# GpSimd arithmetic moved to VectorE, unsplit side tasks, and scores of two heads as 64-row products

## The chip, the core and the metric

One NeuronCore of a Trainium2 chip runs the whole program as one launch. The metric is the device time of that launch in microseconds (us). Engines are named as in the profile: PE is TensorE (PEld its weight loads), DVE is VectorE, ACT is ScalarE, POOL is GpSimd, SP is SyncE, which issues DMAs. "L292" is line 292 of the kernel before.

## The reference, cut

Two blocks over 256 tokens of width 1024, in float32. The first has two layers (a mixer of three kinds of attention, then an MLP of width 4096). The second has a Hyena layer and an attention layer, each followed by 16 experts. What the change touches is in the second block and in what is computed ahead for it:

```python
def hyena_filters(L, w1, b1, w2, b2, w3, freq):        # 64 hidden units
    ...
    h = (h @ w3).reshape(L, HY_ORDER, 2, D_MAIN)       # 2 orders, 2 directions, 768 channels
    h = h * jnp.exp(-t * jnp.abs(deltas))
    h = h / (jnp.sum(jnp.abs(h), axis=(0, 2), keepdims=True) + 1e-6)
    ...                                                # then an FFT of the taps
def memory_cross_attn(cq, mem_n, w_kv):                # 4 heads of 64, 256 memory rows
    mk, mv = jnp.split(mem_n @ w_kv, 2, axis=-1)
    s = jnp.einsum('bqhd,bmhd->bhqm', q, mk) * (HEAD_DIM ** -0.5)
    return jnp.einsum('bhqm,bmhd->bqhd', jax.nn.softmax(s, axis=-1), mv)
def blocked_gqa(q, k, v):                              # 12 query heads of 64 on 4 key heads
    s = jnp.einsum('bqhgd,bkhd->bhgqk', qblk, k) * scale
    return jnp.einsum('bhgqk,bkhd->bqhgd', jax.nn.softmax(s, axis=-1), v)
```

The Hyena layer (`long_conv`) multiplies spectra of 256 tokens with spectra of these filters; both second-block layers add a cross attention over the normalized memory.

## The kernel before, in words

**Stages.** By time in the trace: first mixer to 232 us, its MLP (MLP 0) to 508, second mixer to 752, MLP 1 to 936, Hyena layer to 1086, first experts to 1399, attention layer to 1526, second experts to the end at 1870.8.

**Split products.** Most matrix products run as three passes on a fast number format, fp32r (`mm3`, L304 to L306): each f32 operand is split into hi (rounded, by ACT, L291) and lo (the rest, a subtraction, L292). L292 takes its engine from a cycle: `LO0` in MLP 0 and MLP 1, `LO1` in the Hyena layer, `LO2` in the attention layer's projections, `LO3` in its output projection; all of them alternate between POOL (`G`) and DVE (`V`). The first block's mixers use DVE alone. A few products run in plain f32: the scores and the probabilities of the second block's attention. The trace shows each as two PE instructions.

**Order.** `Pipe.feed` (L112) prepares a unit of weights (load, split) two units ahead of its products; each time a unit has run, `Pipe.tick` (L101) steps every spawned task once. While MLP 0 runs, such a side task computes the filters (`filters_task`, L1063) and then the memory's keys and values (`memory_task`, L1161), and writes them to DRAM (`kd`, `kvd`). A scheduler then reorders instructions on each engine, and every engine works through its own queue in order.

**Filters.** For four parts (order by half of the channels) and two token tiles, two directions each take one product of 128 rows with the weights' hi part and one of 64 rows with the lo part (L1122, L1123) into one PSUM tile `psf`; DVE multiplies by the decay (L1124), POOL adds absolute values into `sab` (L1130), DVE forms sum and difference (L1135), ACT and POOL split them into `hs` (L1136, L1137). PE adds the absolute values up (`psn`, L1142), and three-pass products with the split constant `fFh`, `fFl` give the spectra.

**Memory.** `Norm` (L344 to L373) transposes a tile (`pst`), splits it into `xh` (ACT) and `xl` (DVE, L348), and makes the row of reciprocal norms from `ms`, `nr` and `nrb` (DVE, L360 to L366), which PE spreads over partitions (`psr`, L371). The keys (`psT`) and values (`psM`) are three-pass products fed by the generator `stream`.

**Hyena layer.** Projections as three-pass products, short convolutions on DVE (`ux`, `uv`), then forward transform (`psz`), a complex product with `kd` split into `yh` (ACT) and `yl` (DVE or POOL), inverse transform (`psy`), the gate, and the split output `ah`, `al`; L1372 to L1375, L1380 and L1401 may run on POOL.

**Attention layer.** `main` and `cross_task` run `attend` (L1192) for pairs of heads, in rounds staggered against one another, while PE also does the projections. The keys of a pair stand block-diagonally in `akb` (or `mkb`), 128 rows by two heads of 256 keys, with zeros elsewhere, so that one product of 128 rows by 512 columns gives the scores of both heads for 128 queries (`psl`, L1197). A softmax (`softmax_pair`, L769 to L790) follows, four transposes per key half (`pst`, L1207), and the product with the values (`psv`, L1215). Score, transpose and value tiles share one PSUM pool `B` of four buffers. Rotary turns are on POOL and DVE. The projections run in the order key and last query columns (512 to 1023), cross query, first query columns (0 to 511), values.

## Time and profile before

| | |
|---|---|
| median of 3 runs | 1873.15 us (1870.21 to 1873.5) |
| the profiled execution's own time | 1872.64 us |
| its span in the trace | 1870.8 us |
| mean granted PE clock | 0.959 |
| PE busy | 1628.8 us (87%), 11139 instructions |
| DVE busy | 985.2 us (53%), 1740 |
| ACT busy | 676.6 us (36%), 1118 |
| POOL busy | 315.1 us (17%), 216 |
| DMA in the chain that ended last | 30%, all of it expert weights |

Busy shares are means over stages with different limits: the two expert stages wait for weights, and the mixers and MLPs keep PE busy nearly all the time. So each stage has to be read by itself. The time of an execution is some 2 us more than its span.

### The profile page before, as it was taken

How to read it: one execution, taken by the hardware profiler on the slowest of the kernel's cores; microseconds unless marked ns; L12 is line 12 of the kernel's file. 1: busy time of each engine (PE TensorE's matmuls, PEld its weight loads, DVE VectorE, ACT ScalarE, POOL GpSimd, SP SyncE). 2: the span in 40 equal slices, each digit the busy share in tenths (PEclk: the TensorE clock that was granted, in tenths of full speed). 3: DMA queues.
4: the chain of work that ended last, by engine and by line, in shares of the span. 5: the costliest groups of instructions: out<-in, count | busy, mean ns of one | idle time of the engine just before them, and what ended most of it. 6: DMA issues, size and time to landing. Idle time of an engine off the chain costs nothing. (4 is left out here: it accounts for less than half of the span.)

```text
span 1870.8 us, 27208 instructions
## 1 busy us (share of the span) xinstructions
PE 1628.8 (87%) x11139; PEld 1195.2 (64%) x11139; DVE 985.2 (53%) x1740; ACT 676.6 (36%) x1118; POOL 315.1 (17%) x216
## 2 busy tenths in 40 slices
PE   8999999998999999999989988666667989776765
PEld 7998977788999989999878844212224655221221
DVE  6998686775579977645578752000006862110102
ACT  6446454554454555544445331000003652000001
POOL 1000026654300000444333300000002210000001
PEclk9999999999999999999999988898989999899888
DMA  7543564454644436755244689999998759999997
GB/s 257 160 137 125 172 201 160 164 203 161 209 142 147 130 124 203 278 185 196 99 153 157 254 353 425 425 426 424 426 405 315 272 203 401 425 425 425 425 421 274
DMA packets 136516, 490.41 MB, mean 262 GB/s; under 512 B 11153, under 2 KB 32068, under 8 KB 115912
## 3 DMA queue, kind: packets, MB, share of 16 engines
q1 hardware_dynamic: 135919, 488.11, 69.2%
q8 instruction: 87, 1.43, 0.3%
q10 hardware_dynamic: 472, 0.57, 0.1%
q14 instruction: 38, 0.30, 0.0%
HBM read 483.41 MB, written 5.24 MB: 261 GB/s over the span
## 5 line engine op out<-in xcount | busy, mean ns | idle before, releaser
L291 ACT ACTIVATE hi<-w 128x1024 fp32r<-128x1024 f32 (+3 forms) x330 | 328.0, 997 | 323.7 <-PE psT L306 162.3
L304 PE MATMUL psT<-xh,hi 128*128 128x256 f32 x1328 | 386.8, 291 | 0.9 <-ACT hi L291 0.9
L305 PE MATMUL psT<-xh,lo 128*128 128x256 f32 x1328 | 378.6, 285 | 4.6 <-POOL lo L292 2.7
L306 PE MATMUL psT<-xl,hi 128*128 128x256 f32 x1328 | 378.7, 285 | 0.0
L292 DVE TENSOR_TENSOR lo<-w,hi 128x1024 fp32r<-128x1024 f32 (+3 forms) x245 | 285.3, 1165 | 141.5 <-ACT hi L291 140.6
L292 POOL TENSOR_TENSOR lo<-w,hi 128x1024 fp32r<-128x1024 f32 (+1 forms) x85 | 205.0, 2413 | 590.2 <-ACT hi L291 584.6
L305 PEld LDWEIGHTS psT<-xh,lo 128*128 128x128 f32 x1328 | 256.4, 193 | 9.5 <-POOL lo L292 3.3
L304 PEld LDWEIGHTS psT<-xh,hi 128*128 128x128 f32 x1328 | 256.5, 193 | 9.2 <-issue 6.4
L306 PEld LDWEIGHTS psT<-xl,hi 128*128 128x128 f32 x1328 | 256.1, 193 | 1.4 <-issue 1.1
L1741 PE MATMUL psx<-w,late 128*32 128x256 f32 (+1 forms) x1024 | 154.4, 549 | 75.8 <-DMA w<-in_exp_w_gate 39.5
L1741 PEld LDWEIGHTS psx<-w,late 128*32 128x32 f32 x1024 | 47.1, 116 | 180.5 <-issue 74.9
L1741 PE MATMUL psx<-w,xg 128*32 128x256 f32 (+1 forms) x1024 | 124.3, 547 | 35.2 <-DMA w<-in_exp_w_up 19.7
L1793 PE MATMUL psy<-w,late 128*32 128x512 f32 x576 | 98.8, 601 | 33.7 <-DMA w<-in_exp_w_down 29.8
L1777 ACT ACTIVATE yy<-psy,rslot 128x512 fp32r<-128x512 f32 (+1 forms) x17 | 11.3, 662 | 320.6 <-PE psy L1793 253.7
L1741 PEld LDWEIGHTS psx<-w,xg 128*32 128x32 f32 x1024 | 40.5, 117 | 115.7 <-issue 60.6
L306 PE MATMUL acc<-lo,hh 128*128 128x512 f32 x256 | 100.8, 394 | 3.0 <-POOL lo L292 3.0
L305 PE MATMUL acc<-hi,hlo 128*128 128x512 f32 x256 | 100.8, 394 | 0.0
L304 PE MATMUL acc<-hi,hh 128*128 128x512 f32 x256 | 100.5, 392 | 0.0
L1778 DVE SCALAR_TENSOR_TENSOR yy<-psy,rslot,yy 128x512 fp32r<-128x512 f32 (+1 forms) x17 | 12.2, 720 | 162.0 <-ACT yy L1777 161.5
L1757 DVE TENSOR_TENSOR late<-late,psx 128x512 f32<-128x512 f32 (+1 forms) x16 | 8.1, 550 | 166.3 <-PE psx L1741 166.3
L1793 PEld LDWEIGHTS psy<-w,late 128*32 128x32 f32 x576 | 27.1, 110 | 101.1 <-DMA w<-in_exp_w_down 49.8
L1756 DVE SCALAR_TENSOR_TENSOR late<-psx,rslot,late 128x512 f32<-128x512 f32 (+1 forms) x16 | 9.1, 613 | 152.3 <-ACT late L1755 152.3
(495 smaller groups left out, 2850.1 us busy)
## 6 DMA issues: line engine op xcount, KB each, us to landing
w<-in_exp_w_gate SPq DMA_DIRECT2D x64, 1536.0 KB, 27.6
w<-in_exp_w_up SPq DMA_DIRECT2D x64, 1536.0 KB, 29.5
w<-in_exp_w_down SPq DMA_DIRECT2D x48, 1536.0 KB, 26.9
w<-in_w_in SPq DMA_DIRECT2D x39, 1024.0 KB, 5.2
w<-in_w_up SPq DMA_DIRECT2D x32, 1024.0 KB, 5.6
w<-in_w_down SPq DMA_DIRECT2D x32, 1024.0 KB, 7.1
w<-in_exp_w_down SPq DMA_DIRECT2D x18, 1024.0 KB, 14.2
w<-in_w_out SPq DMA_DIRECT2D x10, 1024.0 KB, 5.6
```

The costliest lines, as they stand in the source:

```text
L291: S.activation(hi, src, AF.Copy)
L292: next(lo_engines[0]).tensor_tensor(lo, src, hi.bitcast(F32), op=ALU.subtract)
L304: PE.matmul(ps, lh, rh, start=start, stop=False)
L305: PE.matmul(ps, ll, rh, start=False, stop=False)
L306: PE.matmul(ps, lh, rl, start=False, stop=stop)
L1741: mm = PE.matmul(pg[nm][n][32 * e:32 * e + 32, :c1 - c0], xg[gr // 2][:, k, 128 * (gr % 2) + 32 * e:128 * (gr % 2) + 32 * e + 32], wt[e][: ...
L1756: V.scalar_tensor_tensor(sg[:, :n], pg["gate"][i][:, :n], r2, sg[:, :n], op0=ALU.mult, op1=ALU.mult)
L1757: V.tensor_tensor(hid[:, c], sg[:, :n], pg["up"][i][:, :n], op=ALU.mult)
L1777: S.activation(yh, py, AF.Copy, scale=rs[:, 2, gr:gr + 1])
L1778: V.scalar_tensor_tensor(yl, py, rs[:, 2, gr:gr + 1], yh.bitcast(F32), op0=ALU.mult, op1=ALU.subtract)
L1793: PE.matmul(py[n][32 * e:32 * e + 32], hT[:, k, 32 * e:32 * e + 32], wt[e][:, k - k0, 512 * n:512 * n + 512], start=k == 0, stop=k == 5, t ...
```

## The change

All `LO` cycles become DVE alone, and so do the Hyena layer's and the attention layer's remaining POOL operations; POOL keeps the routing of the experts and the last output. The side tasks keep their operands in f32: the filter taps become 64-row products, one direction in rows 0 to 63 of the array and one in rows 64 to 127 (`tile_position`), each into its own PSUM tile; the spectra and the memory's keys and values become plain f32 products, and the memory norm makes one f32 tile instead of `xh` and `xl`. In `attend`, one head's keys stand in rows 0 to 63 and the other's in 64 to 127; four products of 64 rows by 256 columns replace two of 128 by 512, and each head gets its own `psl` tile, so the softmax runs per head over both token tiles. The attention layer's first query projection comes before the load of the cross query's and values' weights.

The diff, cut ("LO" lines, `Norm`, `softmax_pair`, filters, memory, `attend`, Hyena layer, attention layer):

```diff
     lo_engines = [cycle((V,))]
-    LO0 = (G, V)
-    LO1 = (G, V)
-    LO2 = (V, G, V)
-    LO3 = (G, V)
+    LO0 = (V,)
...
+            if split is None:
+                self.x = pool.tile([128, 8, T], F32, name="xT")
+            elif split:
                 self.xh = (pool or xtp).tile([128, 8, T], F32R, tag="xh", name="xh")
                 self.xl = (pool or xtp).tile([128, 8, T], F32R, tag="xl", name="xl")
...
+                        S.activation(self.x[:, k], ps[:, j], AF.Copy, scale=self.g[:, k:k + 1])
+                        continue
                     S.activation(self.xh[:, k], ps[:, j], AF.Copy, scale=self.g[:, k:k + 1])
                     V.scalar_tensor_tensor(self.xl[:, k], ps[:, j], self.g[:, k:k + 1], self.xh[:, k].bitcast(F32),
...
-                V.tensor_scalar(nm[:, q:q + 1], nm[:, q:q + 1], scale[q], -1.0, op0=ALU.mult, op1=ALU.mult)
+            V.scalar_tensor_tensor(nm, nm, -1.0, scale, op0=ALU.mult, op1=ALU.mult)
+            scale = [scale[:, q:q + 1] for q in range(2)]
         for q in range(2):
             S.activation(p[:, q], ps[:, q], AF.Exp, bias=nm[:, q:q + 1], scale=scale[q], accum_out=sm[:, q:q + 1])
...
-            Fh = fp.tile([128, 2, 2, 128], F32R, name="fFh")
-            Fl = fp.tile([128, 2, 2, 128], F32R, name="fFl")
-            S.activation(Fh, raw, AF.Copy)
-            V.tensor_tensor(Fl, raw, Fh.bitcast(F32), op=ALU.subtract)
+            F = fp.tile([128, 2, 2, 128], F32, name="fF")
+            nc.sync.dma_start(F, C["fwd"].rearrange("p t (s f) -> p t s f", s=2)[:, :, :, :128])
             yield
...
-            S.activation(hst, h2, AF.Copy)
-            V.tensor_tensor(hst[64:], h2[64:], hst[64:].bitcast(F32), op=ALU.subtract)
...
-                        nc.sync.dma_start(w3[64 * d:64 * d + 64], I["hy_filt_w3_2"][0].rearrange("k (o d c) -> k o d c", o=2, d=2)[:, o, :, c])
...
-                    G.tensor_tensor(w3l, w3[:64], w3h[:64].bitcast(F32), op=ALU.subtract)
-                    hs = {op: [fp.tile([128, 2, 384], F32R, tag=f"h{op}{i}", name="hs") for i in range(2)] for op in (ALU.add, ALU.subtract)}
+                        nc.sync.dma_start(w3[64 * d:64 * d + 64], I["hy_filt_w3_2"][0].rearrange("k (o d c) -> k o d c", o=2, d=2)[:, o, d, c])
+                    hs = {op: fp.tile([128, 2, 384], F32, tag=f"h{op}", name="hs") for op in (ALU.add, ALU.subtract)}
                     sab = fp.tile([128, 384], F32, tag="sab", name="sab")
                     yield
                     for t in range(2):
                         hd = []
+                        sl = slice(t * 128, (t + 1) * 128)
+                        pd = [A("psf", [128, 384]) for _ in range(2)]
+                        for d in range(2):
+                            r = slice(64 * d, 64 * d + 64)
+                            PE.matmul(pd[d], h2[r, sl], w3[r], start=True, stop=True, tile_position=(64 * d, 0))
                         for d in range(2):
                             h = fp.tile([128, 384], F32, tag=f"hd{d}", name="hd")
-                            ps = A("psf", [128, 384])
-                            sl = slice(t * 128, (t + 1) * 128)
-                            PE.matmul(ps, hst[:, sl], w3h[:, d], start=True, stop=False)
-                            PE.matmul(ps, hst[:64, sl], w3l[:, d], start=False, stop=True)
-                            V.tensor_tensor(h, ps, dec[:, t, c], op=ALU.mult)
+                            V.tensor_tensor(h, pd[d], dec[:, t, c], op=ALU.mult)
                             if t == 0 and d == 0:
                                 S.activation(sab, h, AF.Abs)
...
-                                G.tensor_tensor(sab, sab, ab, op=ALU.add)
+                                V.tensor_tensor(sab, sab, ab, op=ALU.add)
                             hd.append(h)
                         yield
                         for op, dst in hs.items():
-                            x = fp.tile([128, 384], F32, tag="hx", name="hx")
-                            V.tensor_tensor(x, hd[0], hd[1], op=op)
-                            S.activation(dst[0][:, t], x, AF.Copy)
-                            G.tensor_tensor(dst[1][:, t], x, dst[0][:, t].bitcast(F32), op=ALU.subtract)
+                            V.tensor_tensor(dst[:, t], hd[0], hd[1], op=op)
...
-                            mm3(pp[t], Fh[:, t, part], Fl[:, t, part], hs[op][0][:, t], hs[op][1][:, t], True, True)
+                            PE.matmul(pp[t], F[:, t, part], hs[op][:, t], start=True, stop=True)
...
             kv = mp.tile([128, 2, 2, T], F32, name="kv")
             w = load(ring, rows_of(I["w_mem_kv_2"][l]))
             yield
-            def put_k(j, ps):
-                V.tensor_tensor(kv[:, 0], ps, nm.R[:, None, :].to_broadcast([128, 2, T]), op=ALU.mult)
-            def put_v(ps):
+            yield
+            ps = A("psT", [128, 2, T])
+            for i in range(2):
+                for q in range(2):
+                    for k in range(4):
+                        PE.matmul(ps[:, q], w[i][:, k, 128 * q:128 * q + 128], nm.x[:, 4 * i + k],
+                                  start=i == 0 and q == 0 and k == 0, stop=i == 1 and q == 1 and k == 3)
+                yield
+            V.tensor_tensor(kv[:, 0], ps, nm.R[:, None, :].to_broadcast([128, 2, T]), op=ALU.mult)
+            ps = [A("psM") for _ in range(2)]
+            for k0 in range(0, 8, 2):
                 for t in range(2):
...
-            yield from stream(dense_M(ring, None, nm.xh, nm.xl, put_v, tiles=[x[:, :, 256:] for x in w]), sp)
+                    for k in (k0, k0 + 1):
+                        PE.matmul(ps[t][:, :256], nm.x[:, k, t * 128:(t + 1) * 128], w[k // 4][:, k % 4, 256:],
+                                  start=k == 0, stop=k == 7)
+                yield
+            for t in range(2):
...
-        kb = pool.tile([128, 2, 2, T], F32, name="mkb")
+        kb = pool.tile([128, 2, 2, T], F32, name="mkb")[:, 0]
         vv = pool.tile([128, 2, 256], F32, name="mvv")
-        G.memset(kb, 0.0)
-        for q in range(2):
-            r = slice(64 * q, 64 * q + 64)
-            nc.sync.dma_start(kb[r, :, q], kvd[r, 0])
+        nc.sync.dma_start(kb, kvd[:, 0])
...
+        ps = [B("psl") for _ in range(2)]
+        for t in range(2):
+            for q in range(2):
+                r = slice(64 * q, 64 * q + 64)
+                PE.matmul(ps[q][:, t], qT[r, t * 128:(t + 1) * 128], kb[r], start=True, stop=True, tile_position=(64 * q, 0))
         p = []
-        for t in range(2):
-            ps = B("psl")
-            PE.matmul(ps, qT[:, t * 128:(t + 1) * 128], kb, start=True, stop=True)
-            pt = pool.tile([128, 2, T], F32, tag="p", name="p")
-            softmax_pair(ps, pt, scale(t), eng)
-            p.append(pt)
+        for q in range(2):
+            p.append(pool.tile([128, 2, T], F32, tag="p", name="p"))
+            softmax_pair(ps[q], p[q], scale(q), eng)
...
-                    PE.transpose(ps[:, q, t * 128:(t + 1) * 128], p[t][:, q, st * 128:(st + 1) * 128], ident)
+                    PE.transpose(ps[:, q, t * 128:(t + 1) * 128], p[q][:, t, st * 128:(st + 1) * 128], ident)
...
-            return attend(cqT[:, j], kv[0][:, j], lambda t: 0.125,
+            return attend(cqT[:, j], kv[0][:, j], lambda q: 0.125,
...
-                G.tensor_tensor(a[0], a[0], a[1], op=ALU.subtract)
+                V.tensor_tensor(a[0], a[0], a[1], op=ALU.subtract)
                 V.tensor_tensor(a[2], a[2], a[3], op=ALU.add)
...
-                    (G if part and not o else V).tensor_tensor(yl[:, b], a[2 * part], yh[:, b].bitcast(F32), op=ALU.subtract)
+                    V.tensor_tensor(yl[:, b], a[2 * part], yh[:, b].bitcast(F32), op=ALU.subtract)
...
-                    (V if n else G).tensor_tensor(al[:, b], sz, ah[:, b].bitcast(F32), op=ALU.subtract)
+                    V.tensor_tensor(al[:, b], sz, ah[:, b].bitcast(F32), op=ALU.subtract)
...
-        G.memset(kb, 0.0)
+        kb = late.tile([128, 2, T], F32, name="akb")
...
-                        G.tensor_tensor(hx(rot[:, t, a:a + 64 * nh])[:, :, :, g], hx(qk[:, t, a:a + 64 * nh])[:, :, :, 1 - g],
+                        V.tensor_tensor(hx(rot[:, t, a:a + 64 * nh])[:, :, :, g], hx(qk[:, t, a:a + 64 * nh])[:, :, :, 1 - g],
...
-                for c in range(2):
-                    V.tensor_copy(kb[0:64, c, 0], ps[0:64, c])
-                    S.activation(kb[64:128, c, 1], ps[64:128, c], AF.Copy)
+                V.tensor_copy(kb, ps)
...
         pipe.feed(dense_M(ring, w_in[:, :, 512:1024], nm.xh, nm.xl, lambda ps: qk_done(1, ps), need=need_r, tiles=wqk or None))
+        pipe.feed(dense_M(ring, w_in[:, :, 0:512], nm.xh, nm.xl, lambda ps: qk_done(0, ps)))
         w = load(ring, w_in[:, :, 1024:1536])
         kv = memory_load(pool, kvd)
...
         def cq_done(j, ps):
-            while nm.R is None:
-                pipe.tick()
...
         ct = pipe.spawn(cross_task(kv, cqT, late, lambda: "cq" in done, lambda: box.get("a"), E2))
         pipe.feed(dense_T(ring, None, nm.xh, nm.xl, cq_done, tiles=[x[:, :, 256:] for x in w]))
-        pipe.feed(dense_M(ring, w_in[:, :, 0:512], nm.xh, nm.xl, lambda ps: qk_done(0, ps)))
         pipe.spawn(main())
         pipe.feed(dense_M(ring, None, nm.xh, nm.xl, v_done, tiles=[x[:, :, :256] for x in w]))
```

**PE in MLP 0, a filter group between the products of the MLP** (`psT` is the MLP's, `psf` the filters'). Before:

```order
L306 MATMUL psT_3196<-xl_2787,hi_3114 128x256
L1122 MATMUL psf_3222<-fw3h_3183,fhst_3090 128x384
L1123 MATMUL psf_3222<-fw3l_3184,fhst_3090 128x384
L1122 MATMUL psf_3228<-fw3h_3183,fhst_3090 128x384
L1123 MATMUL psf_3228<-fw3l_3184,fhst_3090 128x384
L304 MATMUL psT_3196<-xh_2786,hi_3147 128x256
```

Now:

```order
L304 MATMUL psT_3183<-xl_2787,hi_3140 128x256
L1103 MATMUL psf_3208<-fw3_3173,fh2_3085 128x384
L1103 MATMUL psf_3209<-fw3_3173,fh2_3085 128x384
L302 MATMUL psT_3183<-xh_2786,hi_3140 128x256
L303 MATMUL psT_3183<-xh_2786,lo_3141 128x256
```

Four filter products in two tiles became two, one to a tile, at the same kind of place.

**DVE at the start of the Hyena layer**, where the last of MLP 1's sums (`X`), the norm (`ss`, `ms`, `nr`, `rt`) and the first weights' `lo` meet. Before:

```order
L994 SCALAR_TENSOR_TENSOR X<-acc,r_8105,X 128x512 x2
L355 SCALAR_TENSOR_TENSOR junk,ss<-X 128x512
L360 TENSOR_TENSOR ms<-ss 128x2
L361 TENSOR_SCALAR ms<-ms 128x2
L312 TENSOR_SCALAR nr<-ms 128x2
L313 TENSOR_SCALAR rh<-ms 128x2
L321 TENSOR_TENSOR rt<-rh,nr 128x2
L292 TENSOR_TENSOR lo<-w,hi 128x1024
```

Now:

```order
L998 SCALAR_TENSOR_TENSOR X<-acc,r_7789,X 128x512 x2
L359 SCALAR_TENSOR_TENSOR junk,ss<-X 128x512
L290 TENSOR_TENSOR lo<-w,hi 128x1024 x3
L352 SCALAR_TENSOR_TENSOR xl<-pst,cols,xh 128x256 x2
L364 TENSOR_TENSOR ms<-ss 128x2
L1406 TENSOR_TENSOR invl<-w,invh 128x1024
```

Three lo parts now stand ahead of the norm's chain on DVE.

**PE late in the attention layer**: scores (`psl`), transposes (`pst`) and values (`psv`) of the head pairs between the products of the output projection (`psO`). Before:

```order
L304 MATMUL psO<-hl,ah 128x512
L305 MATMUL psO<-hl,al 128x512
L306 MATMUL psO<-hl,ah 128x512
L1215 MATMUL psv<-pT,avv 64x256 x4
L1207 MATMUL pst<-ident,p 128x128 x8
L1197 MATMUL psl<-akb,aqT 128x512 x2
```

Now:

```order
L302 MATMUL psO<-hl,ah 128x512
L303 MATMUL psO<-hl,al 128x512
L1194 MATMUL pst<-ident,p 128x128 x4
L304 MATMUL psO<-hl,ah 128x512
L1183 MATMUL psl<-akb,aqT 128x256 x4
L1202 MATMUL psv<-pT,avv 64x256 x4
L1194 MATMUL pst<-ident,p 128x128 x2
```

A pair's scores are four shorter products, and they stand ahead of the transposes that they followed.

## Rows read from the trace of the kernel before

**Rows 1.** Windows: us; busy of PE, PEld, DVE, ACT, POOL; PEclk; DMA; GB/s.
```profile
232.00:508.00 276.00, 258.36 (x1586) 225.31 (x1585) 183.59 (x222) 137.24 (x199) 134.68 (x71) 0.99 0.54 183
752.00:936.00 184.00, 183.36 (x1179) 166.89 (x1178) 101.22 (x102) 90.81 (x113) 75.36 (x32) 1.00 0.54 186
936.00:1086.00 150.00, 134.66 (x906) 123.03 (x904) 116.27 (x200) 68.26 (x132) 52.80 (x39) 0.98 0.56 202
...
1436.00:1513.00 77.00, 72.73 (x369) 49.04 (x368) 62.46 (x169) 47.55 (x120) 21.06 (x25) 0.96 0.63 231
```

**Rows 2.** The chain that ended last: start, us, what.
```profile
1065.02 1.02 POOL ya L1375
...
1129.95 29.69 DMA w<-in_exp_w_gate
...
1479.12 0.86 PE psl L1197 x2
...
1487.16 1.20 ACT p L781 x4
```

**Rows 3.** Groups of L292 in MLP 1: duration ns min/median/max, first and last start.
```profile
L292 POOL TENSOR_TENSOR lo<-w,hi x31: 2386/2401/2413, 753.2 to 923.9; 128x1024 fp32r<-128x1024 f32 x31
L292 DVE TENSOR_TENSOR lo<-w,hi x31: 1211/1224/1227, 758.9 to 926.6; 128x1024 fp32r<-128x1024 f32 x31
```

**Rows 4.** Timeline at the Hyena layer's start: start, us, engine, line, operation.
```profile
936.12 4.96 POOL L292 TENSOR_TENSOR lo<-w,hi 128x1024 fp32r<-128x1024 f32 x2 [8.96 <-ACT hi L291]
936.54 2.19 DVE L360 TENSOR_TENSOR ms<-ss 128x2 f32<-128x2 f32 x1
...
941.41 0.16 DVE L321 TENSOR_TENSOR rt<-rh,nr 128x2 f32<-128x2 f32 x1
```

**Rows 5.** PE's waits, 235 to 512 us: total us, times, longest.
```profile
PE pst L344 <- DVE xl L348: 4.8, 1, 4.8
PE acc L306 <- POOL lo L292: 3.0, 4, 0.8
PE psf L1122 <- DVE fhst L1097: 2.1, 1, 2.1
PE psn L1142 <- POOL sab L1130: 2.1, 3, 0.9
```

**Rows 6.** Windows as in Rows 1, after the longest wait of Rows 5.
```profile
430.00:435.00 5.00, 5.00 (x34) 5.00 (x33) 3.10 (x6) 2.33 (x6) 0.00 (x0) 0.72 0.49 148
```

**Rows 7.** Timeline of PE: a filter group; three-pass products of 256 columns.
```profile
276.37 0.45 PE L1122 MATMUL psf<-fw3h,fhst 128*128 128x384 f32 x1 [2.11 <-DVE fhst L1097]
276.75 0.44 PE L1123 MATMUL psf<-fw3l,fhst 64*128 64x384 f32 x1
...
277.86 0.39 PE L304 MATMUL psT<-xh,hi 128*128 128x256 f32 x1
...
460.01 0.28 PE L305 MATMUL psM<-hi,xl 128*128 128x256 f32 x1
460.13 0.28 PE L306 MATMUL psM<-lo,xh 128*128 128x256 f32 x1
```

**Rows 8.** PE's waits in the Hyena layer, 936 to 1086 us.
```profile
PE psr L371 <- DVE nrb L366: 3.3, 1, 3.3
PE pst L1352 <- DVE ux L1404: 3.0, 3, 1.5
PE psT L305 <- POOL lo L292: 1.3, 1, 1.3
```

**Rows 9.** PE's waits in the attention layer, 1426 to 1526 us.
```profile
PE psl L1197 <- DVE cqT L1546: 2.5, 1, 2.5
PE pst L1501 <- DVE qp L1493: 1.7, 2, 1.4
PE psT L305 <- POOL lo L292: 1.4, 1, 1.4
```

**Rows 10.** Windows as in Rows 1, where the first experts begin.
```profile
1100.00:1105.00 5.00, 4.85 (x29) 1.83 (x32) 1.67 (x3) 1.59 (x3) 0.00 (x0) 0.50 0.06 15
```

More of the change, by code (lines that the diff above doesn't have):

```diff
@@ L1031, in wait @@
             yield
-    def stream(units, pool):
-        ahead = deque()
-        for u in units + [None, None]:
-            if u:
-                hl.append(pool)
-                u.prep()
-                hl.pop()
-                ahead.append(u)
-            if len(ahead) == 3 or not u:
-                ahead.popleft().run()
-            yield
     def sin_layer(ps, b, fr, out, pool):
@@ L1091, in filters_task @@
             h2 = fp.tile([128, T], F32, name="fh2")
-            hst = fp.tile([128, T], F32R, name="fhst")
             ps = A("psf", [128, T])
@@ L1159, in filters_task, with memory_task @@
             V.reciprocal(rn, nrm)
-    def memory_task(ring, mp, sp, m, kvd):
-        nm = Norm(m, gain("mem_norm_g_2"), mp, A)
+    def memory_task(ring, mp, m, kvd):
+        nm = Norm(m, gain("mem_norm_g_2"), mp, A, None)
         yield from nm.task(lambda n: True)
@@ L1168, in memory_task @@
             yield
-            def put_k(j, ps):
-                V.tensor_tensor(kv[:, 0], ps, nm.R[:, None, :].to_broadcast([128, 2, T]), op=ALU.mult)
-            def put_v(ps):
-                for t in range(2):
-                    evac(kv[:, 1, t], ps[t][:, :256], t, nm.r[:, t:t + 1])
-            yield from stream(dense_T(ring, None, nm.xh, nm.xl, put_k, tiles=[x[:, :, :256] for x in w]), sp)
-            yield from stream(dense_M(ring, None, nm.xh, nm.xl, put_v, tiles=[x[:, :, 256:] for x in w]), sp)
+            yield
[9 more added lines that the diff above has]
+            for k0 in range(0, 8, 2):
+                for t in range(2):
+                    for k in (k0, k0 + 1):
[3 more added lines that the diff above has]
+            for t in range(2):
+                evac(kv[:, 1, t], ps[t][:, :256], t, nm.r[:, t:t + 1])
             nc.sync.dma_start(kvd[l], kv)
     def memory_load(pool, kvd):
-        kb = pool.tile([128, 2, 2, T], F32, name="mkb")
+        kb = pool.tile([128, 2, 2, T], F32, name="mkb")[:, 0]
         vv = pool.tile([128, 2, 256], F32, name="mvv")
-        G.memset(kb, 0.0)
-        for q in range(2):
-            r = slice(64 * q, 64 * q + 64)
-            nc.sync.dma_start(kb[r, :, q], kvd[r, 0])
+        nc.sync.dma_start(kb, kvd[:, 0])
         nc.sync.dma_start(vv, kvd[:, 1])
@@ L1441, in attention_layer @@
         tg = c2["tg"]
-        kb = late.tile([128, 2, 2, T], F32, name="akb")
-        G.memset(kb, 0.0)
+        kb = late.tile([128, 2, T], F32, name="akb")
         qk = pool.tile([128, 2, 1024], F32, name="qk")
@@ L1835, in mlp0_tasks @@
         yield from filters_task(ring, kd)
-        with tc.tile_pool(name="memp", bufs=1) as mp, tc.tile_pool(name="mems", bufs=3) as sp:
+        with tc.tile_pool(name="memp", bufs=1) as mp:
             m = mp.tile([128, 2, D], F32, name="mem")
@@ L1840, in mlp0_tasks @@
                 yield
-            yield from memory_task(ring, mp, sp, m, kvd)
+            yield from memory_task(ring, mp, m, kvd)
     c2s = ctx
```

12 lines of the change are left out of this document (5 added, 7 removed).

## Prediction

> **What bounds the kernel now.** I read the busy time by stage first, then the chain of waits, then for each stage the waits of PE. In MLP 1 PE is busy for 183.36 of 184 us, so nothing that other engines do faster can help there. In MLP 0, the Hyena layer and the attention layer PE idles for 276.00 - 258.36 = 17.6, 150.00 - 134.66 = 15.3 and, in the 77 us with head pairs, 4.3 us [rows 1]: there is the room. In the attention layer DVE is nearly as full: 62.46 of 77 us. The experts are bounded by their weights: one piece of the chain is 29.69 us of waiting for a gate's weights [rows 2]. Ahead of the first experts the DMA share falls to 0.06 for 5 us [rows 10], that is, the weight buffers were full and the loads waited for the experts to begin. So I let time that is saved ahead of the experts pass through to the end.
>
> **GpSimd's subtractions move to VectorE.** One 128x1024 subtraction takes POOL 2.40 us and DVE 1.22 us, a ratio of 0.51 [rows 3]. POOL's work also slows DVE down: beside two of them, DVE's additions of 2x128 numbers take 2.19 us, where the same kind of step takes 0.16 afterwards [rows 4]. So the move adds less to DVE than it seems. In MLP 0, DVE would be at 183.59 + 0.51 x 134.68 = 252.3 of 276 us at the very most, in MLP 1 at 101.22 + 0.51 x 75.36 = 139.7 of 184 [rows 1]. I cost both at nothing on the path; PE's own products are the cover. If that cover is gone, each late lo costs what POOL's late ones cost in MLP 0, up to 3.0 / 4 = 0.75 us [rows 5].
>
> **MLP 0 with the side tasks.** Here PE is the engine that counts, since its idle time is scattered.
>
> - *Filter taps.* Eight groups. Before, a group takes 277.86 - 276.37 = 1.49 us for four products, 0.37 each, in which 128-row and 64-row products alternate. A three-pass product of 256 columns follows its neighbour after 0.12 us, so 384 columns should take 0.18; changing between the two heights costs 0.19 each time [rows 7]. Now there are two plain f32 products of 64 rows. A plain product of 512 columns is two PE instructions in 0.86 us [rows 2], so one of 384 takes 0.64. Side by side they take 0.64 and two changes of height 0.4, in all 1.04; one after the other 1.68. No row shows two such products side by side. They touch different rows of the array and different PSUM tiles, so I take 1.04: 8 x (1.04 - 1.49) = **-3.6**; the other end is 8 x 0.19 = +1.5.
> - *Spectra.* 48 three-pass products of 384 columns at 0.18 become 16 plain ones at 0.64: 10.2 - 8.6 = **+1.6**.
> - *Keys and values of the memory.* 192 passes of 256 columns at 0.12 = 23.0 become 64 plain products at 0.43 = 27.5: **+4.5**.
> - *Waits of PE* [rows 5]. The 3.0 us for POOL's lo go, as DVE does it in half the time. Of the 2.1 us for `sab`, 0.6 stay, as DVE still adds. The 4.8 us for `xl` fall to 0.8: the memory's transposes wait for one ACT copy alone. The 2.1 us for `fhst` fall to 1.0, since ACT's sine layer stays. Together 3.0 + 1.5 + 4.0 + 1.1 = **-9.6**.
> - *The clock.* In the 5 us after the longest of these waits PE is granted 0.72 of its clock [rows 6], a mixture of the levels 1.2 and 2.4 GHz. Without that idle time 5 x 0.28 = **-1.4** comes back.
>
> The DMA of F is one more load on SP's queue and takes a ring load away; the four stored parts go as before. Sum for MLP 0: -3.6 + 1.6 + 4.5 - 9.6 - 1.4 = **-8.5**.
>
> A row first: a 64-row product behind a 128-row one takes 0.37 where 0.18 was expected [rows 7]. The Trainium skill, page "TensorEngine Tiling (Array Packing)", section "Key Properties", says that a change of tiling mode drains the engine, and that tiles then load and multiply independently. The row agrees with the first; no run here shows the second. By that rule the pair costs 1.04, by the serial end 1.68.
>
> **Hyena layer.** (1) The start. DVE's chain from `ms` to `rt` begins at 936.54, and its first `rt` is at 941.41, since two tiny operations on the way are slow beside POOL's two subtractions; one that took 2.19 takes 0.16 otherwise, so some 2 x 2.1 = 4.2 us would go [rows 4]. Now three lo parts stand ahead of the chain where one stood in it: 2 x 1.22 = 2.4 back [rows 3]. So the row of norms comes 1.8 earlier. PE's 3.3 us for `nrb` [rows 8] may go altogether, as 24 more products of 0.12 now stand ahead of `psr`, but DVE's convolutions need that row too and are late next: 1.8. With the 1.3 us for POOL's lo [rows 8] that is **-3.1**. (2) `ya` on POOL stands in the chain with 1.02 us [rows 2]; at the ratio above 0.52, twice: **-1.0**. (3) Of PE's 3.0 us for `ux` [rows 8], DVE's queue gives back a third, no longer held by POOL: **-1.0**, between 0 and -3.0. (4) Two score pairs: before, 2 x 0.86 = 1.72; now two steps of two products side by side, 2 x 0.43, with 0.4 for the changes of height, 1.25: 2 x -0.47 = **-0.9**; one after the other a pair would take 2.11. Added to DVE: 0.51 x 52.80 = 26.9 to 116.27 of 150 us [rows 1]. That fits only on the average, and is the ground of rival D. Sum **-6.0**.
>
> **Attention layer.** The waits that could go are 2.5 for `cqT`, 1.7 for `qp` and 1.4 for POOL's lo [rows 9], and eight pairs at 0.47 are 3.8 more: 9.4 in all. But DVE takes over 0.51 x 21.06 = 10.7 us and stands at 73.2 of 77 us [rows 1], so no more than 3.8 us can go in that window. With half the 1.4 us for the lo, which stands before it, **-4.5**. Fewer softmax operations (one for both scales, one copy of the keys, no zero filling) and the reordered projections I put at nothing: the `q` half ahead of the cross query fills the time in which PE waited for `cqT`, and that is counted. If PE then waits for the later cross query, 2.5 is the price.
>
> **Elsewhere** nothing: the first block's mixers have no POOL work, and the experts follow their weights. The sum stands against the profiled execution's own 1872.64 us, 0.5 below the median: 1872.64 - 8.5 - 6.0 - 4.5 = **1853.6**. Its own range is 1846 to 1862: half of what rival C adds (-5.4), and above, half of the waits I let go in MLP 0 (+4.8) with the start of the Hyena layer lost (+3.1).
>
> **Rivals.**
>
> - *C, the freed VectorE gives more.* All the waits listed go: in MLP 0 2.4 more, in the Hyena layer 3.3 + 3.0 + 1.3 + 1.0 + 0.9 = 9.5, in the attention layer 9.4: 1872.64 - 10.9 - 9.5 - 9.4 = 1842.8. For it speaks how far tiny operations were slowed; against it, that DVE is at 73 of 77 us.
> - *B, the 64-row halves run one after another*, so that part of the change doesn't do what it says. Filters +5.1 against my sum; Hyena pairs 2 x 0.86 = +1.7; in the attention layer PE would stand at 72.73 + 8 x 0.39 = 75.9 of 77, a gain of 1.1 instead of 3.8: +2.7. 1863.1.
> - *F, two score tiles are held at once.* A pair now takes two of four `B` buffers until the softmax of its second head has been read, while transposes and values want them too. Before, the next score tile came after the exponentials of the one before, 1.20 us in the chain [rows 2]. One such wait in each of six staggered rounds: 7.2, so 1860.8. The Trainium skill, page "TensorEngine Tiling (Array Packing)", section "Gotcha 1: PSUM Pressure", says that row tiles must write to different PSUM banks and so need more of them; no run here shows the effect.
> - *E, the weight stream absorbs what is saved in the second block*, because loads, not buffers, set the experts' begin: only MLP 0's 8.5 stay, 1864.1. Against it speaks the DMA share of 0.06 [rows 10].
> - *D, slower: VectorE's queue becomes the bound in the Hyena and attention layers.* It works in order, so a subtraction for a weight two units ahead can stand before a convolution, a maximum or a normalization for which PE waits. It takes over 26.9 + 10.7 = 37.6 us. If half falls on the path, 18.8 - 8.5 = +10.3: 1882.9. It decides for slower from 8.5 + 3.75 = 12.2 us, a third of 37.6. For it speaks the order at the Hyena layer's start, where three lo parts go ahead of the norm; against it, that POOL's work slowed DVE before.
>
> **How the numbers follow.** Chances: the forecast 0.45, C 0.13, B 0.10, F 0.10, E 0.11, D 0.11. The likeliest gives 1853.6. The range 1840 to 1869 holds all but D (0.11) and the outer ends of C, E and B together (0.07): E with F's wait on top would pass 1869. A measurement of this kernel can tell about 0.2%, 3.7 us. Faster 0.84: all but D and the 0.05 in which losses of B, E and F come together. Within 0.2%: those 0.05 and 0.02 of D, 0.07. Slower: the other 0.09 of D.
>
> **What would show it.** In the changed kernel's trace: the waits of PE for POOL's lo and for `xl` in MLP 0 gone and its stage some 8 us shorter; the two products of a filter group beginning nearly together (forecast) or 0.6 us apart (B); the first `nr` steps of the Hyena layer at 0.2 us each, and that stage 6 us shorter; DVE at about 73 us in the window of the head pairs, with that window some 4 us shorter; no wait of `psl` or `pst` for a buffer (F would show them, released by ACT's `p`); the experts' stages as long as before (E would show DMA waits grown by 10). It is wrong above all if the small waits listed are replaced by waits for DVE in the same places.

## The result and the profile after

The changed kernel takes 1828.26 us (median of 4 runs, 1824.88 to 1828.49) against 1873.33, a ratio of 0.9759 (0.9742 to 0.9776): 45 us faster. The forecast was 1853.6, a gain of 19, with a range of 1840 to 1869; the sign was right and the size less than half of what came. The profiled execution took 1824.88 us, with a span of 1823.1.

Stage by stage, in the two profiled executions, from the last product of one stage to the last of the next (us). The first mark is put at 232.00 us in both, and the attention layer begins with its first product; the marks given with the stages of the kernel before were round numbers. The gains add up to the 47.7 us between the two spans:

| stage | before | changed | forecast gain | measured gain |
|---|---|---|---|---|
| first mixer and second mixer | 232.0, 243.2 | 232.0, 243.0 | 0 | 0.2 |
| MLP 0 with the side tasks | 277.1 | 255.8 | 8.5 | 21.3 |
| MLP 1 | 182.6 | 182.6 | 0 | 0 |
| Hyena layer | 149.5 | 130.4 | 6.0 | 19.1 |
| attention layer | 110.0 | 102.1 | 4.5 | 7.9 |
| both expert stages | 330.3, 346.1 | 331.3, 345.9 | 0 | -0.8 |

The windows view by stage (us; busy of PE, PEld, DVE, ACT, POOL; granted clock; DMA share; GB/s), MLP 0, MLP 1, Hyena and attention layer, of the kernel before at these marks:

```profile
232.00:509.06 277.06, 259.42 (x1591) 226.19 (x1590) 184.65 (x223) 137.24 (x199) 134.68 (x71) 0.99 0.54 182
752.26:934.91 182.65, 182.64 (x1175) 166.58 (x1174) 100.02 (x100) 89.52 (x111) 75.36 (x32) 1.00 0.54 184
934.91:1084.45 149.54, 133.58 (x894) 121.80 (x893) 115.66 (x198) 67.88 (x130) 52.70 (x38) 0.98 0.56 202
1414.72:1524.75 110.03, 102.66 (x498) 70.18 (x499) 80.91 (x205) 60.85 (x142) 31.57 (x32) 0.95 0.70 260
```

And of the changed kernel:

```profile
232.00:487.79 255.79, 255.77 (x1511) 219.95 (x1510) 163.07 (x251) 118.98 (x166) 0.10 (x1) 1.00 0.57 193
...
730.76:913.36 182.60, 182.59 (x1175) 166.61 (x1174) 107.67 (x131) 89.53 (x110) 0.00 (x0) 1.00 0.54 187
913.36:1043.80 130.44, 127.91 (x903) 118.26 (x901) 113.74 (x229) 68.28 (x130) 0.52 (x3) 1.00 0.63 231
...
1375.10:1477.21 102.11, 98.45 (x530) 70.18 (x531) 79.80 (x217) 60.03 (x140) 0.93 (x5) 0.99 0.74 279
```

In MLP 0 PE now has no idle time at all, where it had 17.6 us. In the Hyena layer its idle time went from 149.54 - 133.58 = 16.0 to 2.5 us. DVE's column is the surprise: in the Hyena layer it executes 229 instructions instead of 198 for the same stage, and is busy for 113.74 us instead of 115.66. In MLP 1 it executes 31 subtractions of 1.23 us more, 38 us, and its busy time grows by 7.65 (from 100.02).

One operation shows why. These are the groups of DVE's subtraction `hlo` in MLP 1, an operation that the change doesn't touch (busy us, mean ns; idle time before); the kernels are the one before, then the changed one:

```profile
L1012 DVE TENSOR_TENSOR hlo<-r,hh 128x512 fp32r<-128x512 f32 x16 | 37.7, 2359 | 11.5 <-ACT hh L1009 11.5
```
```profile
L1016 DVE TENSOR_TENSOR hlo<-r,hh 128x512 fp32r<-128x512 f32 x16 | 11.0, 686 | 0.0
```

The same 16 operations take 26.7 us less. In the kernel before, 15 of them begin while a subtraction of GpSimd runs, and one that meets none takes 0.69 us. In the Hyena layer the same holds for one of the two steps of the short convolution: 12 operations at 1052 ns before and at 481 now. (The other step follows right behind it on DVE, meets no operation of GpSimd, and takes 472 ns before.)

```profile
L1333 DVE SCALAR_TENSOR_TENSOR ux<-tmp,sw,ux 128x255 f32<-128x255 f32 x12 | 12.3, 1052 | 2.7 <-ACT ux L1332 2.7
...
L1371 DVE TENSOR_TENSOR ya<-psz,kf 128x384 f32<-128x384 f32 x8 | 4.4, 550 | 0.2
```
```profile
L1320 DVE SCALAR_TENSOR_TENSOR ux<-tmp,sw,ux 128x255 f32<-128x255 f32 x12 | 5.3, 481 | 0.7 <-ACT ux L1319 0.7
...
L1358 DVE TENSOR_TENSOR ya<-psz,kf 128x384 f32<-128x384 f32 x8 | 4.4, 552 | 0.0
```

The products with a spectrum (`ya<-psz,kf`), which read one operand from PSUM, took 550 ns before and take 552 now: they were not held up. Of the 32 of them, 11 began while GpSimd was at work, and these took 541 to 557 ns too. What remains of PE's waits in the Hyena layer of the changed kernel (total us, times, longest), against [rows 8]:

```profile
PE pst L345 <- DVE X L998: 0.6, 1, 0.6
PE psy L302 <- ACT yh L1366: 0.5, 1, 0.5
PE psy L303 <- DVE yl L1367: 0.4, 1, 0.4
PE psr L375 <- DVE nrb L370: 0.3, 1, 0.3
```

### The profile page after: what moved, and what is told of

Its sections match the earlier page's. It is cut to its first block, busy times and chain, and to the rows that moved or that the text cites. A ratio compares the mean times of both kernels' runs of the same rounds, so it can differ in the third digit from the quotient of the medians.

```text
span 1823.1 us, 26914 instructions
## 1 busy us (share of the span) xinstructions
PE 1616.1 (89%) x11099; PEld 1184.6 (65%) x11099; DVE 969.8 (53%) x1845; ACT 658.1 (36%) x1082; POOL 20.9 (1%) x53
## 4 chain that ended last, share of the span: by engine, by line
PE 61%; DMA 29%; DVE 5%; ACT 2%; issue 1%; SPq 1%; ACTq 0%; DVEq 0%
DMA w<-in_exp_w_up 10%; DMA w<-in_exp_w_gate 10%; DMA w<-in_exp_w_down 9%; PE psT L302 8%; PE psT L303 8%; PE psT L304 8%; PE acc L302 3%; PE acc L303 3%; PE acc L304 3%; PE psM L302 3%; PE psM L303 3%; PE psM L304 3%; PE psx L1723 2%; SPq L187 1%; DVE lo L290 1%
## 5 line engine op out<-in xcount | busy, mean ns | idle before, releaser
L290 DVE TENSOR_TENSOR lo<-w,hi 128x1024 fp32r<-128x1024 f32 (+3 forms) x318 | 368.1, 1159 | 167.8 <-ACT hi L289 164.1
L289 ACT ACTIVATE hi<-w 128x1024 fp32r<-128x1024 f32 (+3 forms) x318 | 320.0, 1007 | 374.6 <-PE psT L304 166.5
L302 PE MATMUL psT<-xh,hi 128*128 128x256 f32 x1296 | 375.1, 290 | 1.0 <-ACT hi L289 1.0
L303 PE MATMUL psT<-xh,lo 128*128 128x256 f32 x1296 | 367.0, 283 | 1.2 <-DVE lo L290 1.2
L304 PE MATMUL psT<-xl,hi 128*128 128x256 f32 x1296 | 366.4, 283 | 0.0
L302 PEld LDWEIGHTS psT<-xh,hi 128*128 128x128 f32 x1296 | 247.6, 191 | 11.4 <-issue 8.7
L303 PEld LDWEIGHTS psT<-xh,lo 128*128 128x128 f32 x1296 | 247.9, 191 | 5.4 <-DVE lo L290 1.9
L304 PEld LDWEIGHTS psT<-xl,hi 128*128 128x128 f32 x1296 | 247.7, 191 | 0.7 <-issue 0.7
L302 PE MATMUL acc<-hi,hh 128*128 128x512 f32 x256 | 104.6, 408 | 0.0
L1737 ACT ACTIVATE late<-psx,rslot 128x512 f32<-128x512 f32 (+1 forms) x16 | 8.4, 577 | 203.7 <-PE psx L1723 177.1
```

Source lines behind the costliest of these rows:

```text
L289: S.activation(hi, src, AF.Copy)
L290: next(lo_engines[0]).tensor_tensor(lo, src, hi.bitcast(F32), op=ALU.subtract)
L302: PE.matmul(ps, lh, rh, start=start, stop=False)
L303: PE.matmul(ps, ll, rh, start=False, stop=False)
L304: PE.matmul(ps, lh, rl, start=False, stop=stop)
L1737: S.activation(sg[:, :n], pg["gate"][i][:, :n], AF.Sigmoid, scale=r1)
```

## The experiments

Theory L: GpSimd's arithmetic held VectorE up for about as long as VectorE now needs for the same work; the gain is the end of that. Rivals: U, the gain comes from the unsplit side tasks and shorter scores; W, GpSimd's results merely came late; B, F, O and others on single parts.

**VectorE alone takes over.** In the kernel before:

```diff
-    LO0 = (G, V)
...
+    LO0 = (V,)
...
-                                G.tensor_tensor(sab, sab, ab, op=ALU.add)
+                                V.tensor_tensor(sab, sab, ab, op=ALU.add)
```
and likewise for the other `LO` cycles, `fw3l`, `hs`, `ya`, `yl`, `al` and `rot`.

> The kernel before with one part of the change alone: all its subtractions, products and sums on GpSimd in the MLPs, the side tasks, the Hyena layer and the attention layer go to VectorE. Side tasks stay split, scores stay block-diagonal, the projections keep their order. Theory L (GpSimd's work cost VectorE as much time as VectorE now spends on it, because VectorE's operations were held up beside it): the Hyena layer falls from 149.6 to about 132 us, the attention layer from 110.1 to about 105, MLP 0 from 277.1 to about 267, in all about 1840. VectorE's busy time in the Hyena layer stays within 5 us of 115.7. Rival U (the gain needs the unsplit side tasks and the shorter scores, which make room on VectorE): MLP 0 stays above 274, the Hyena layer above 140, in all 1858 or more. Rival D (VectorE's queue becomes the bound): slower than 1873.

Measured: 1830.79 us, ratio 0.978 (0.9761 to 0.9798). MLP 0 260.0, Hyena layer 131.3, attention layer 104.8:

```profile
232.00:491.96 259.96, 257.51 (x1597) 226.79 (x1596) 187.58 (x294) 137.97 (x200) 0.10 (x1) 0.99 0.58 195
...
917.49:1048.76 131.27, 128.81 (x894) 118.35 (x893) 113.86 (x229) 68.47 (x130) 0.53 (x3) 1.00 0.63 229
...
1377.91:1482.74 104.83, 101.06 (x498) 69.19 (x499) 83.02 (x230) 60.62 (x142) 3.22 (x7) 0.97 0.72 270
```

That part alone gives 42 of the 45 us. VectorE's busy time in MLP 0 rose by 2.9 us (from 184.65) for 71 operations more. Theory L's numbers came in both layers; in MLP 0 it had 267 and in all 1840, and more was gained. U and D fall.

**The other parts without it.** The changed kernel with the `LO` cycles, `sab`, `ya`, `yl`, `al` and `rot` as before:

```diff
-    LO0 = (V,)
-    LO1 = LO2 = LO3 = (V,)
+    LO0 = (G, V)
+    LO1 = (G, V)
+    LO2 = (V, G, V)
+    LO3 = (G, V)
```

> The changed kernel with the GpSimd arithmetic put back (the weights' lo in the order of the kernel before, sab, ya, yl, al and the rotary turns), all else as changed. Theory L: the Hyena layer goes back to about 147 us from 130.4, the attention layer to about 108 from 102.1, MLP 0 to about 263 from 255.8, MLP 1 unchanged at 182.6; in all about 1858. Rival U: MLP 0 stays within 2 us of 255.8 and the Hyena layer within 6 of 130.4; in all under 1840.

Measured: 1855.18 us (0.9908, 0.9889 to 0.9926). MLP 0 261.0, Hyena layer 149.3, attention layer 109.5. These are near theory L's numbers, and U's fall. In the two layers nothing is left of the gain. In MLP 0 either part alone gives most of it, 17.1 (VectorE alone) or 16.1 (unsplit alone), and both together 21.3. The two overlap, since the unsplit side tasks also take work from GpSimd: it is busy there for 92.49 us with 45 operations, 134.68 with 71 before. So in this stage their share is not told apart from the end of the hold-up; in the layers they have none.

**GpSimd works, and nobody reads what it writes.** The changed kernel, in `split`, for the units that GpSimd had before:

```diff
         next(lo_engines[0]).tensor_tensor(lo, src, hi.bitcast(F32), op=ALU.subtract)
+        if next(dup[0]):
+            ...
+            G.tensor_tensor(s, src, hi.bitcast(F32), op=ALU.subtract)
```

> The changed kernel in which GpSimd computes again those lo parts of weights that it computed in the kernel before, into a scratch tile that nobody reads; VectorE computes all that are used, as in the changed kernel. No engine waits for a result of GpSimd. Theory L (VectorE is held up beside GpSimd's work): VectorE's busy time grows though it executes the same instructions, by 20 us or more over MLP 1, and the Hyena layer grows by 6 to 15 us; in all 1838 to 1850. Rival W (what counted were results that came late from GpSimd): all stages within 1 us of the changed kernel's, in all within 0.2% of 1828.

Measured: 1877.02 us, ratio 1.002 (1.001 to 1.003), slower than the kernel before; the profiled execution took 1869.68. VectorE's `hlo` in MLP 1 is back near the mean of the kernel before (12 of them take 2.90 us, the other 4 0.69), and its `lo` are longer too (1605 ns). That group comes first; then a stretch of DVE's and of POOL's timeline (start, us) shows how operations that stand side by side in the profile take turns:

```profile
L1028 DVE TENSOR_TENSOR hlo<-r,hh 128x512 fp32r<-128x512 f32 x16 | 37.5, 2343 | 0.0
```
```profile
809.73 1.23 DVE L293 TENSOR_TENSOR lo<-w,hi 128x1024 fp32r<-128x1024 f32 x1 [0.25 <-ACT hi L292]
810.87 2.90 DVE L1028 TENSOR_TENSOR hlo<-r,hh 128x512 fp32r<-128x512 f32 x1
```
```profile
809.83 3.39 POOL L299 TENSOR_TENSOR scr<-w,hi 128x1024 bf16<-128x1024 f32 x1 [3.06 <-ACT hi L292]
```
```profile
751.08 2.41 POOL L299 TENSOR_TENSOR scr<-w,hi 128x1024 bf16<-128x1024 f32 x1 [5.35 <-issue]
```

POOL's subtraction starts just after DVE's `lo`, which ends at 810.96, and ends itself at 813.22, 2.26 us later; the last line shows that such a one takes 2.41 us when no long operation of DVE stands before it. So GpSimd is held up as well. The small `hlo` behind it ends at 813.77, 0.55 us after POOL's subtraction and so by about its own time. And the windows of MLP 1 and of the Hyena layer:

```profile
742.34:927.03 184.69, 183.34 (x1175) 166.54 (x1174) 158.78 (x132) 89.89 (x110) 96.88 (x31) 1.00 0.52 182
927.03:1079.07 152.04, 134.57 (x902) 122.85 (x901) 136.82 (x229) 68.68 (x130) 43.23 (x23) 0.97 0.53 190
```

DVE is busy 51 us longer in MLP 1, yet that stage grows by 2.1 us only, since PE is its bound; in the Hyena layer 23 us more of DVE cost 21.6 us of the stage. W can't explain it: none of these results is read. Their reading keeps weight buffers from being filled again (the queue that issues the loads waited for them, 16.3 us in MLP 1 and 8.0 in the Hyena layer), but PE's waits in the Hyena layer have another source, VectorE. The longest (total us, times, longest):

```profile
PE psT L312 <- DVE lo L293: 4.0, 2, 2.4
PE psr L384 <- DVE nrb L379: 2.9, 1, 2.9
```

None is for GpSimd or a load. In the kernel before, PE's waits for a result of GpSimd itself were 3.0 + 2.1 us in MLP 0, 1.3 in the Hyena layer and 1.4 in the attention layer ([rows 5], [rows 8], [rows 9]), 7.8 in all: W's direct share of the gain is at most that. The size was more than expected, probably as VectorE has all its own work here and the hold-ups besides; no run separates this.

**Which of GpSimd's work.** The changed kernel with only the weights' lo parts back on GpSimd, and with only the small operations back.

```diff
-    LO1 = LO2 = LO3 = (V,)
+    LO1 = (G, V)
```

> The changed kernel with only the weights' lo parts back on GpSimd (the four LO cycles as before); sab, ya, yl, al and the rotary turns stay on VectorE. With all of it back the Hyena layer took 149.3 us, the attention layer 109.5, MLP 0 261.0. Theory L1 (each microsecond of GpSimd's work in a stage costs alike, since it holds VectorE up): lo parts are 37.1 of 52.7 us of GpSimd's time in the Hyena layer, so it takes 130.4 + 0.7 x 18.9 = 143 to 144 us; the attention layer 106 to 108; MLP 0 260; in all about 1850. Rival P (what counts is work in the chain from product to product: ya, yl, al): the Hyena layer stays under 137 us, in all under 1842.

```diff
-                V.tensor_tensor(a[0], a[0], a[1], op=ALU.subtract)
+                G.tensor_tensor(a[0], a[0], a[1], op=ALU.subtract)
```

> The changed kernel with only sab, ya, yl, al and the rotary turns back on GpSimd; the weights' lo parts stay on VectorE. Theory L1: 14.6 of 52.7 us of GpSimd's time in the Hyena layer, so 130.4 + 0.3 x 18.9 = 136 us; MLP 0 within 2 of 255.8; the attention layer 103 to 105; in all about 1836. Rival P: the Hyena layer takes 141 us or more.

Measured: 1851.61 us (0.9887, 0.986 to 0.9915) and 1832.02 (0.9783, 0.976 to 0.9806). The Hyena layer took 149.1 with the lo parts and 135.2 with the small operations:

```profile
918.09:1067.18 149.09, 132.86 (x903) 121.33 (x901) 122.25 (x213) 67.69 (x130) 37.25 (x23) 0.98 0.56 203
914.44:1049.62 135.18, 130.01 (x903) 118.55 (x901) 111.87 (x214) 68.15 (x130) 16.26 (x20) 1.00 0.62 222
```

P falls, and so does the proportion of L1: the lo parts alone bring the stage back to what all of it cost (149.3). The two costs, 18.7 and 4.8 us, overlap and don't add up to the 18.9 of both.

**One operand or two.** The unread work again, as a copy:

```diff
-            G.tensor_tensor(s, src, hi.bitcast(F32), op=ALU.subtract)
+            G.tensor_copy(s, src)
```

> The kernel with GpSimd's unread second lo parts, with one edit: GpSimd copies the weights into the scratch tile (one operand read) where it subtracted (two operands read). With the subtraction MLP 0 took 267.4 us, the Hyena layer 152.0 and the attention layer 112.9, and VectorE was busy for 158.8 us in MLP 1 with the same instructions for which it is busy 107.7 in the changed kernel. Theory T (GpSimd's operations on two tensors hold VectorE up, copies don't): VectorE's busy time in MLP 1 is within 5 us of 107.7, the Hyena layer within 2 of 130.4, in all within 0.3% of 1828. Rival A (any work of GpSimd on memory holds it up): VectorE is busy for over 125 us in MLP 1, in all over 1845.

Measured: 1841.18 us (0.9831, 0.9808 to 0.9853); DVE busy 114.57 us in MLP 1, the Hyena layer 135.3, the attention layer 106.5. Neither theory's numbers. The hold-up per us of POOL's work in MLP 1 is (114.57 - 107.67) / 41.06 = 0.17, against (158.78 - 107.67) / 96.88 = 0.53 for the subtraction. Yet a copy holds VectorE up until its end just as a subtraction does, as the first two of these lines from that stage show (start, us):

```profile
746.80 1.18 POOL L299 CAST scr<-w 128x1024 bf16<-128x1024 f32 x1 [2.04 <-DMA w<-in_w_up]
746.99 1.52 DVE L1028 TENSOR_TENSOR hlo<-r,hh 128x512 fp32r<-128x512 f32 x1
792.83 1.04 POOL L299 CAST scr<-w 128x1024 bf16<-128x1024 f32 x1 [4.82 <-DMA w<-in_w_up]
```

The `hlo` ends 0.53 us behind the copy's end at 747.98; so T's ground, that copies don't hold VectorE up, falls. The copies are cheaper since each is over sooner (1.04 us alone, in the last line, against 2.41) and since fewer meet: they start earlier, when the weights land, and 2 of the 16 `hlo` take 1.52 us, where 12 took 2.90. How much each of the two gives stays open.

**Are the halves side by side?** Both products of each pair on rows 0 to 63:

```diff
-                            r = slice(64 * d, 64 * d + 64)
-                            PE.matmul(pd[d], h2[r, sl], w3[r], start=True, stop=True, tile_position=(64 * d, 0))
+                            r = slice(0, 64)
+                            PE.matmul(pd[d], h2[r, sl], w3[r], start=True, stop=True, tile_position=(0, 0))
```
and the same in `attend`.

> The changed kernel in which both products of each pair (filter taps and scores) take rows 0 to 63 of the array, the first direction's and the first head's operands, so that two of them cannot run side by side; it computes the first direction and the first head twice instead of both. The order of instructions is the same on each engine. Theory S (the two halves run side by side in the changed kernel): a filter group takes 0.64 us more, MLP 0 grows by 8 x 0.64 = 5.1 us, the two pairs of the Hyena layer 0.86 each, 1.7, the eight of the attention layer up to 6.9; in all 1836 to 1842. Rival B (they run one after another anyway): all stages within 1 us, in all within 0.2% of 1828.

Measured: 1837.46 us (0.9814, 0.9799 to 0.9828). MLP 0 261.6, Hyena layer 131.8, attention layer 107.3; in runs that share the changed kernel's MLP 0 it took 255.8 to 257.3. A filter group and the product behind it on PE, in the changed kernel and in this one:

```profile
277.20 0.92 PE L1103 MATMUL psf<-fw,fh 64*128 64x384 f32 x4
278.05 0.38 PE L302 MATMUL psT<-xh,hi 128*128 128x256 f32 x1
```
```profile
272.85 1.55 PE L1103 MATMUL psf<-fw,fh 64*128 64x384 f32 x4
274.33 0.39 PE L302 MATMUL psT<-xh,hi 128*128 128x256 f32 x1
```

0.85 us against 1.48, a difference of 0.63: one whole product of 384 columns. They do run side by side; B falls. The Trainium skill, page "TensorEngine Tiling (Array Packing)", section "Key Properties", says that tiles work independently; for two halves of 64 rows, these two rows show it.

**Scores as before.** The changed kernel with the block-diagonal `attend`:

```diff
-                PE.matmul(ps[q][:, t], qT[r, t * 128:(t + 1) * 128], kb[r], start=True, stop=True, tile_position=(64 * q, 0))
+            PE.matmul(ps, qT[:, t * 128:(t + 1) * 128], kb, start=True, stop=True)
```

> The changed kernel with the scores as before: block-diagonal keys with zeros, two products of 128 rows by 512 columns a pair, softmax per token tile; all else as changed. Theory S (a pair side by side takes 0.47 us less of TensorE, and nothing else of it matters): the Hyena layer grows by 0.9 us, the attention layer by up to 3.8 (eight pairs), in all 1830 to 1833. Rival F (two score tiles at once cost waits): the attention layer is no longer than 102.1, in all 1828 or less. Rival M (the work on the mask, the zeros and the keys' copies matters more): the attention layer grows by over 4.

Measured: 1829.82 us (0.9772, 0.9757 to 0.9786); Hyena layer 131.2, attention layer 105.6. The stages fit S (0.8 and 3.5 us longer; 2.2 against the 103.4 us that the changed kernel's attention layer took in its second profile); F falls: two score tiles at once cost nothing that shows, and PE has no wait of `psl` or `pst` for ACT's `p` in the changed kernel's attention layer. In the whole time the intervals overlap with the changed kernel's.

**The order of the projections**, put back in the changed kernel, first alone and then beside the changed kernel on one chip:

```diff
-        pipe.feed(dense_M(ring, w_in[:, :, 0:512], nm.xh, nm.xl, lambda ps: qk_done(0, ps)))
         w = load(ring, w_in[:, :, 1024:1536])
...
+        pipe.feed(dense_M(ring, w_in[:, :, 0:512], nm.xh, nm.xl, lambda ps: qk_done(0, ps)))
         pipe.spawn(main())
```

> The changed kernel with the attention layer's projections in the order of the kernel before (cross query before the first query columns). Theory O (the order removes TensorE's wait of 2.5 us for the cross query's DVE result, as the trace of the changed kernel shows no such wait): the attention layer grows by 2 to 3 us from 102.1, in all about 1831. Rival N (with a free VectorE the wait is gone in either order): within 1 us, in all within 0.1% of 1828.

> The changed kernel with the attention layer's projections in the order of the kernel before, once more beside the changed kernel itself, since the difference was 2 us. If the order of the change costs time, as the attention stage suggests (99.9 against 102.1 us), this is 1 to 3 us faster than the changed kernel on the same chip; if the difference was chance, both are within 0.1%.

> The changed kernel itself, as the measure for the run with the other order: 1825 to 1829.

Measured: 1826.17, then 1824.55 us (0.9742, 0.9729 to 0.9755) beside 1828.22 (0.9759, 0.9745 to 0.9774). The attention layer takes 99.9 and 100.7 us against 102.1 and 103.4. So the new order gains nothing and costs 2 to 3 us of its stage; why, no run shows. The wait for `cqT` is gone in either order, as rival N had it, though neither rival had the stage shorter. This version is the fastest that was measured; by whole times its lead over the changed kernel, 3.7 us, is as small as a measurement can tell.

**The rest of the routing on VectorE**, on top of that order:

```diff
-        for k in range(2):
-            lo(k, G)
...
+        for k in range(2):
+            lo(k, V)
```

> The changed kernel with the attention layer's projections in the order of the kernel before and with the routing's two lo parts and the small cast moved from GpSimd to VectorE, behind the router's probabilities. In the changed kernel TensorE waits 0.8 and 0.3 us for these lo parts. Theory V (the same hold-up, in small): each expert stage begins up to 1 us earlier, in all 1 to 2 us under the run with the order alone (1826.2). Rival N: the lo parts only change places in VectorE's queue: no difference beyond 0.1%.

Measured: 1826.14 us (0.9753, 0.9738 to 0.9767), no gain over the order alone, as its rival N had it.

## Why the prediction was right in sign and wrong in size

- **The failed step** is the price on VectorE. The prediction took VectorE's recorded busy time for work and added the moved work to it, "0.51 x 52.80 = 26.9" in the Hyena layer and "0.51 x 21.06 = 10.7 us" in the attention layer, though that time already held the hold-ups. In the sum this is the cap of 3.8 us on the attention layer and the ground of rival D; elsewhere the end of the hold-up counted only in the few waits that were named. The durations of [rows 4] were a sign of the hold-up, and I used them at the Hyena layer's start alone. With VectorE alone taking over, its busy time changed by +2.9 us in MLP 0, +7.7 in MLP 1, -1.8 in the Hyena layer and +2.1 in the attention layer. So DVE was no limit, and the cap (7.9 came in that stage) and rival D had no ground. In the window of the head pairs, at the same distances from the stage's ends, DVE is busy for 57.62 of 69.00 us where about 73 were forecast:

```profile
1396.40:1465.40 69.00, 66.76 (x391) 47.90 (x390) 57.62 (x172) 45.87 (x117) 0.93 (x5) 1.00 0.61 228
```

- **The waits of PE** are where it shows in the sum. I let 9.6 of 17.6 us go in MLP 0, and did not list 3.6 for `nrm` and 2.0 for `fh`; all went (PE's waits in MLP 0 that [rows 5] leaves out; total us, times, longest):

```profile
PE psf L304 <- DVE nrm L1143: 3.6, 4, 0.9
PE psf L1094 <- ACT fh L1061: 2.0, 1, 2.0
```

  With VectorE alone taking over, both are gone as well. That it was the small DVE operations behind them that were held up is argued, not shown one by one. In the Hyena layer I let 1.8 + 1.3 + 1.0 + 1.0 = 5.1 us go; of 16.0, 13.4 went. Rival C, which came nearest with 1842.8, listed the right cause but still only some of the waits.
- **PE's own time.** For the unsplit side tasks the sum had -3.6 + 1.6 + 4.5 = +2.5 us. With VectorE alone in both kernels, PE is busy in MLP 0 for 255.77 us with them and 257.51 without, -1.7 (granted clock 1.00 and 0.99). Of the three terms, the filter groups' was too dear: 8 x (0.85 - 1.49) = -5.1, not -3.6. For the other two it is not shown.
- **The clock** was counted only in MLP 0 (-1.4). The Hyena layer had such a stretch too: the granted clock from 949 to 969 us was 0.83, between the levels of 1.2 and 2.4 GHz, behind the idle times of its start, and in the changed kernel's same stretch it is 1.00, the upper level. 20 x 0.17 = 3.4 us, an estimate, came back that the sum left out. PE's busy time for the same 894 products of the whole stage fell by 4.8, from 133.58 to 128.81 with VectorE alone:

```profile
949.00:969.00 20.00, 16.94 (x111) 16.59 (x112) 11.57 (x20) 7.68 (x14) 3.73 (x3) 0.83 0.46 158
```
```profile
927.90:947.90 20.00, 19.86 (x153) 19.51 (x152) 18.11 (x35) 11.35 (x20) 0.00 (x0) 1.00 0.24 81
```

- **Right:** that the halves run side by side (0.85 us a group where 1.04 was forecast, 0.63 dearer in series), nothing in MLP 1 and the mixers, and that the experts neither gain nor absorb: B, E and F fell by their own numbers.
- **Right by luck in part:** the start of the norm's row. `nrb` began 14.9 us into the Hyena layer before and 12.5 now, 2.4 earlier where 1.8 was forecast. But the chain from `ms` to `nrb` became 13.28 - 6.77 = 6.5 us shorter, not 4.2 (a third of its steps, an `rt` of 2.33 us at 947.07, was held up too), and began 5.7 us into the stage instead of 1.6, 4.1 later, not 2.4. Before (the first `ms` is in [rows 4]), then now:

```profile
938.77 2.33 DVE L361 TENSOR_SCALAR ms<-ms 128x2 f32<-128x2 f32 x1
...
949.82 0.29 DVE L366 COPY nrb<-nr 128x256 f32<-128x256 f32 x1
```
```profile
919.07 0.15 DVE L364 TENSOR_TENSOR ms<-ss 128x2 f32<-128x2 f32 x1
...
925.84 0.29 DVE L370 COPY nrb<-nr 128x256 f32<-128x256 f32 x1
```

- **Wrong in detail:** the order of the projections was put at nothing or a gain of a filled wait; it costs 2 to 3 us. The lower end of the forecast's own range, 1846, is a slip: half of what rival C adds leads from 1853.6 to 1848. Nothing hangs on it, as the measured time lies below both, and below the 1840 of the wider range.

## What to carry to other kernels

Before arithmetic is shared between GpSimd and VectorE, compare VectorE's mean duration of one unchanged operation with and without GpSimd at work: a busy VectorE may be a held-up one. A busy time can't be added to as if it were work; price a move by a kernel that leaves the other engine idle, or by one that gives it unread work. Whether the hold-up matters is then a question of the stage: 51 us of it cost 2 us where TensorE was the bound, and 23 us cost 21.6 where small VectorE steps stood between products.
